# Second parts of the w_in weights from an adding transfer, in a hybrid delta-net and attention layer

## The chip, the cores and the metric

The kernel runs on one core of a Trainium2 chip. The metric is the device time of one execution in microseconds; lower is better. The core has a matrix engine (TensorE, PE in the profile; its weight loads are PEld), VectorE (DVE), ScalarE (ACT), GpSimd (POOL) and SyncE (SP), which issues most transfers. GpSimd and ScalarE can issue transfers too. Each engine works through its own queue in order.

## What is computed

One decoder layer for 1024 tokens of width 1024. A combined projection feeds two head groups, a gated delta rule and a differential attention; their outputs are projected back, and a gated feed-forward block follows.

```python
proj = rms_norm(h, norm1_w[l]) @ w_in[l]
dq, dk, dv, dz, da, db, fq, fk, fv = jnp.split(proj, IN_SPLITS, axis=-1)
qkv = jax.nn.silu(causal_dwconv(jnp.concatenate([dq, dk, dv], axis=-1), dn_conv_w[l]))
...
o_a = gated_delta_rule(q_a, k_a, v_a, g_a, beta_a).astype(h.dtype)
...
o_b = diff_attention(q_b, k_b, v_b, lam)
...
mix = jnp.concatenate([o_a.reshape(B_, S_, DN_V), o_b.reshape(B_, S_, DF_V)], axis=-1)
h = h + mix @ w_out[l]
u = causal_dwconv(rms_norm(h, norm2_w[l]) @ w_up[l], ffn_conv_w[l], ffn_conv_b[l])
gate, up = jnp.split(u, 2, axis=-1)
h = h + (jax.nn.silu(gate) * up) @ w_down[l]
```

## The kernel before, in words

Every large product is made of float32 operands split into two parts. The first part, `hi`, is a copy rounded to float32r (ScalarE, L202); the second part, `lo`, is what the rounding left, raw - hi. A product is then three matmuls: hi by hi, hi by lo, lo by hi. The normed input is split once into `xn`; the weights are split as they are loaded.

`split_w` makes the two parts of a loaded weight tile `raw` of 128 x 1024. With `lo_eng` G, GpSimd subtracts (L204); otherwise VectorE does (L206). `load_w128` loads one block of 128 columns of w_in (512 KB) and `gemm_T` uses it: two output halves of 512 tokens, eight k steps each, three matmuls per step (L422 and L423 read hi, L424 reads lo). `load_wn` loads 256 columns as two raw tiles of four k steps each, and `proj_nat` uses them: eight row blocks of 128 tokens, for each sixteen matmuls with hi (L403, L404) and then eight with lo (L406). Two row blocks share one PSUM tile, and there are two such tiles.

The order of use is this: the three blocks of head 0 of the delta group by `proj_T` (two of them loaded ahead into `pre`), then nine more by `delta_proj` for heads 1 to 3, then seven calls of `proj_nat` by 256 columns: one for dz ("dz1"), one for q and k of attention head 0, one for v, and four as `filler` within attention head 0. Between them, on the same engines, run the delta group's own chains: conv4 (L570 on ScalarE, three L573 on VectorE, L575 silu on ScalarE), the transposes L611, the scores L638 and L639, a triangular inverse by steps of VectorE (L684 to L687), and the scan over chunks (`delta_scan`, L754 to L776), in which TensorE, VectorE and ScalarE wait for each other in turn.

The weight parts `hi` and `lo` come from the pool wp with five buffers; a buffer comes free with TensorE's last matmul of the weight that it held. `raw` has three buffers; one comes free when both parts are made, and the next load on SP's queue waits for that.

The order of the instructions on each engine is written by a planner at build time: it goes by the priorities in `PRI` and by its own model of how long each instruction takes and when buffers come free. On the chip each engine keeps to that order.

The lines that the steps speak of, in `split_w`, are these (the functions around them follow):

```python
S.activation(hi, raw[:, 0:w], AF.Copy)
if lo_eng is G:
    G.tensor_tensor(lo, raw[:, 0:w], hi.bitcast(F32), op=ALU.subtract)
```

Of the kernel before, what the change touches and what calls it, by code (L numbers as in the profile page):

```python
# [10 lines left out]
F32 = mybir.dt.float32  # L11
# [3 lines left out]
AF = mybir.ActivationFunctionType  # L15
ALU = mybir.AluOpType
AX = mybir.AxisListType

P = 128
# [39 lines left out]
def hybrid_layer(ctx, tc, x, positions, norm1_w, w_in, dn_conv_w, dn_a_log, dn_dt_bias,  # L59
# [2 lines left out]
                 ffn_conv_b, w_down, cst, out, dbg=None, stop=None):  # L62
    nc = tc.nc
    V, S, G, PE = nc.vector, nc.scalar, nc.gpsimd, nc.tensor
    dbg = dbg or {}

    cp = ctx.enter_context(tc.tile_pool(name="cp", bufs=1))
# [14 lines left out]
    @contextmanager  # L82
    def part(name):
        p = tc.cur_priority
        q = max(0, p - PRI[name])
        tc.cur_priority = q
        yield
        tc.cur_priority = p + tc.cur_priority - q
# [3 lines left out]
    def nm(s):  # L92
        uid[0] += 1
        return f"{s}_{uid[0]}"
# [4 lines left out]
    def gtr(s):  # L99
        return gt(s, dt=F32R)  # L100

    def jt(s, dt=F32):
        return jp.tile([P, T], dt, tag="j", name=nm(s))

    def ct_(s, dt=F32):
        return cq.tile([P, T], dt, tag="c", name=nm(s))
# [13 lines left out]
    def psG(s="pG"):  # L120
        return pq.tile([P, 512], F32, tag="G", name=nm(s), bufs=2)
# [16 lines left out]
    win = w_in.rearrange("l d c -> (l d) c")  # L138
# [61 lines left out]
    def split_w(raw, lo_eng=None, w=T, alloc=None):  # L200
        hi, lo = ((alloc or wt)(s)[:, 0:w] for s in ("whi", "wlo"))
        S.activation(hi, raw[:, 0:w], AF.Copy)  # L202
        if lo_eng is G:
            G.tensor_tensor(lo, raw[:, 0:w], hi.bitcast(F32), op=ALU.subtract)  # L204
        else:
            V.tensor_tensor(lo, raw[:, 0:w], hi.bitcast(F32), op=ALU.subtract)  # L206
        return hi, lo

    def load_w128(w, c0, lo_eng=None, after=None):

        raw = rp.tile([P, T], F32, tag="raw", name=nm("raw"))
        if after is not None:
            G.tensor_copy(raw[:, 0:1], after)
        nc.sync.dma_start(raw.rearrange("p (k c) -> p k c", c=P),
                          w[:, c0:c0 + P].rearrange("(k p) c -> p k c", p=P))
        hi, lo = split_w(raw, lo_eng)
        return (hi.rearrange("p (k c) -> p k c", c=P), lo.rearrange("p (k c) -> p k c", c=P))

    def load_wn(srcs, lo_eng=None, kg=4, alloc=None, after=None):


        wd = sum(w for _, _, w in srcs)
        parts = []
        for k0 in range(0, NK, kg):
            n = min(kg, NK - k0)
            raw = rp.tile([P, T], F32, tag="raw", name=nm("raw"))
            if after is not None:
                V.tensor_copy(raw[:, 0:1], after)
            rv = raw[:, 0:n * wd].rearrange("p (k c) -> p k c", c=wd)
            o = 0  # L230
            for w, c0, w_ in srcs:
                nc.sync.dma_start(
                    rv[:, :, o:o + w_],
                    w[k0 * P:(k0 + n) * P, c0:c0 + w_].rearrange("(k p) c -> p k c", p=P))
                o += w_
            hi, lo = split_w(raw, lo_eng, n * wd, alloc)
            parts.append((hi.rearrange("p (k c) -> p k c", c=wd),
                          lo.rearrange("p (k c) -> p k c", c=wd)))
        return lambda kt: (parts[kt // kg][0][:, kt % kg, :], parts[kt // kg][1][:, kt % kg, :])
# [39 lines left out]
    def new_xn():  # L279

        return [tuple(xp.tile([P, 4 * T], F32R, tag="xn", name=nm("xn")) for _ in range(2))
                for _ in range(2)]

    def xs(xn, part, kt, a, b):
        q = a // 512
        return xn[q][part][:, kt * 512 + a - q * 512:kt * 512 + b - q * 512]
# [13 lines left out]
    xn = new_xn()  # L300
# [3 lines left out]
    with tc.manual_schedule(engines={mybir.EngineType.Activation}):  # L304
        for tt in range(NT + 1):
# [7 lines left out]
            if 0 < tt < 4:  # L313
                k = tt - 1
                n = min(3, NK - 3 * k)
                hi, lo = (gtr("w0")[:, 0:n * 264].rearrange("p (k c) -> p k c", c=264) for _ in range(2))
# [70 lines left out]
    def proj_nat(srcs, dst, lo_eng=None, extra=None):  # L387


        wf = load_wn(srcs, lo_eng, 4) if extra is None else lambda kt: tuple(t[:, kt % 3, :] for t in srcs[kt // 3])  # L390
        npt = 1 if extra is not None else 2
        for q in range(2):
            st = jt("pn")
            for t0 in range(0, 4, npt):
                ps = psG("pn")
                for i in range(npt):
                    tt = q * 4 + t0 + i
                    a, b = tt * P, tt * P + P
                    w = 264 if extra is not None else 256
                    o = ps[:, i * w:(i + 1) * w]  # L400
                    for kt in range(NK):
                        wh, wl = wf(kt)
                        PE.matmul(o, xs(xn, 0, kt, a, b), wh, start=kt == 0, stop=False)  # L403
                        PE.matmul(o, xs(xn, 1, kt, a, b), wh, start=False, stop=False)  # L404
                    for kt in range(NK):
                        PE.matmul(o, xs(xn, 0, kt, a, b), wf(kt)[1], start=False, stop=kt == NK - 1)  # L406
                if extra is not None:
                    V.tensor_copy(extra[:, tt, :], ps[:, 256:264])
                S.activation(st[:, t0 * 256:(t0 + npt) * 256], ps[:, 0:npt * 256], AF.Copy)
                yield  # L410
            nc.sync.dma_start(
                pn_dram[q * 512:(q + 1) * 512, dst:dst + 256].rearrange("(t p) c -> p t c", p=P),
                st.rearrange("p (t c) -> p t c", c=256))

    def gemm_T(w, c0, x_, ps, lo_eng, qq=(0, 1)):

        whi, wlo = pre.pop(c0 // P, None) or load_w128(w, c0, lo_eng)
        for q in qq:
            qs = (q * 512, q * 512 + 512)
            o = ps(q)  # L420
            for kt in range(NK):
                PE.matmul(o, whi[:, kt, :], xs(x_, 0, kt, *qs), start=kt == 0, stop=False)  # L422
                PE.matmul(o, whi[:, kt, :], xs(x_, 1, kt, *qs), start=False, stop=False)  # L423
                PE.matmul(o, wlo[:, kt, :], xs(x_, 0, kt, *qs), start=False, stop=kt == NK - 1)  # L424
            yield q, o
# [3 lines left out]
    def proj_T(h, kind):  # L429
        ct = kind * 4 + h  # L430
        st = praw[ct] = ct_("pT")
        for q, o in gemm_T(win, ct * P, xn, lambda q: psG("gT"), G):
            S.activation(st[:, q * 512:(q + 1) * 512], o, AF.Copy)
            yield

    def steps(gen, n=99):
        for _ in range(n):
            if next(gen, gen) is gen:
                break

    nat0 = proj_nat(wf0, 0, extra=dab)
    head0 = [proj_T(0, kind) for kind in (1, 0, 2)]
    steps(nat0, 4)
    steps(head0[0], 1)
# [18 lines left out]
    for bits in (8, 8, 8):  # L463
        e = math.floor(math.log2(abs(rest)))
        q = 2.0 ** (e - bits + 1)
# [115 lines left out]
    def load_rows(h):  # L581
        dec = gt("dec")
        nc.sync.dma_start(dec, G_dram[h:h + 1, :].broadcast_to([P, T]))
        return dec
# [379 lines left out]
                              og.rearrange("p (t c) -> p t c", c=P))  # L964

    def qk_proj(h):
        return proj_nat([(win, 2056 + h * P, P), (win, 2568 + h * P, P)], 512 + h * 256, G)

    def v_proj(pr):
        return proj_nat([(win, 3080 + pr * 256, 256)], 1536 + pr * 256, G)  # L970

    def delta_proj(h):
        for kind in (1, 0, 2):
            steps(proj_T(h, kind))

    def delta_end(d):
        with part("dscan"):
            delta_scan(d)
        with part("dout"):
            delta_out(d)  # L980

    ds_ = []
    for h in range(4):
        dec = load_rows(h)
        if h > 0:
            with part("dproj"):
                delta_proj(h)
            if h == 3:
                with part("dz1"):
                    steps(proj_nat([(win, 1792, 256)], 256, G))  # L990
        with part("dprep"):
            ds_.append(delta_prep(h, dec))
        if h > 0:
            delta_end(ds_[h - 1])
        with part("dinv"):
            delta_inverse(ds_[h])
# [8 lines left out]
    with part("qk0"):  # L1005
        steps(qk_proj(0))
# [5 lines left out]
    def load_wo(k0, c, eng, alloc=None):  # L1012

        parts = []
        for i in range(2):
            raw = rp.tile([P, T], F32, tag="raw", name=nm("raw"))
            r0 = (k0 + 2 * i) * P
            nc.sync.dma_start(raw.rearrange("p (k c) -> p k c", c=512),
                              wout[r0:r0 + 2 * P, c * 512:(c + 1) * 512].rearrange("(k p) c -> p k c", p=P))
            parts.append(split_w(raw, eng, T, alloc))  # L1020
        return lambda k: tuple(t[:, (k % 2) * 512:(k % 2) * 512 + 512] for t in parts[k // 2])
# [379 lines left out]
```

## Time and profile before

| | |
|---|---|
| median of 3 runs | 1429.08 us (1425.96 to 1431.47) |
| the profiled execution, its own time | 1430.1 us |
| its span, first to last instruction | 1428.4 us |
| mean granted TensorE clock | 0.975 |
| busy: PE, DVE, ACT, POOL | 1334.5, 878.3, 611.3, 377.0 us |
| wlo<-raw,whi on POOL (L204) | 34 instructions, 83.8 us |
| whi<-raw on ACT (L202) | 58 instructions, 61.0 us |

The span lies 1.7 us under the execution's own time. A busy time is the time in which an engine works on an instruction, whether or not anything waits for it; idle time of an engine that is not the bottleneck costs nothing. Times in the rows are counted from the start of the span.

### The profile page before, as it was taken

How to read it: one execution, taken by the hardware profiler on the slowest of the kernel's cores; microseconds unless marked ns; L12 is line 12 of the kernel's file. 1: busy time of each engine (PE TensorE's matmuls, PEld its weight loads, DVE VectorE, ACT ScalarE, POOL GpSimd, SP SyncE). 2: the span in 40 equal slices, each digit the busy share in tenths (PEclk: the TensorE clock that was granted, in tenths of full speed). 3: DMA queues.
4: the chain of work that ended last, by engine and by line, in shares of the span. 5: the costliest groups of instructions: out<-in, count | busy, mean ns of one | idle time of the engine just before them, and what ended most of it. 6: DMA issues, size and time to landing. Idle time of an engine off the chain costs nothing. (4 is left out here: it accounts for less than half of the span.)

```text
span 1428.4 us, 20608 instructions
## 1 busy us (share of the span) xinstructions
PE 1334.5 (93%) x7927; PEld 1126.6 (79%) x7927; DVE 878.3 (61%) x1745; ACT 611.3 (43%) x1086; POOL 377.0 (26%) x295
## 2 busy tenths in 40 slices
PE   7998898989989998999887999999999989999998
PEld 6876676888989986778665788888888868888887
DVE  5467978886342368867787666666666656334321
ACT  6445454533325365665554444444444435222220
POOL 3044313131242245240022434444333420000000
PEclk8999999999999999999998999999999999999999
DMA  7231112031543267455331222222222247547421
GB/s 225 83 80 35 34 39 75 17 113 66 162 109 116 88 169 192 105 134 162 123 121 29 89 74 89 85 78 89 89 74 82 82 137 243 195 149 229 139 88 59
DMA packets 143393, 155.14 MB, mean 109 GB/s; under 512 B 9279, under 2 KB 114367, under 8 KB 143295
## 3 DMA queue, kind: packets, MB, share of 16 engines
q1 hardware_dynamic: 130815, 144.14, 31.8%
q0 software_dynamic: 11008, 8.39, 3.1%
q8 instruction: 62, 1.02, 0.3%
q10 hardware_dynamic: 1472, 1.29, 0.3%
q14 instruction: 36, 0.29, 0.1%
HBM read 111.32 MB, written 38.29 MB: 105 GB/s over the span
## 5 line engine op out<-in xcount | busy, mean ns | idle before, releaser
L385 PE MATMUL pd<-whi,gl 128*128 128x512 f32 x352 | 137.0, 389 | 0.0
L383 PE MATMUL pd<-whi,gh 128*128 128x512 f32 x352 | 137.0, 389 | 0.0
L384 PE MATMUL pd<-wlo,gh 128*128 128x512 f32 x352 | 137.0, 389 | 0.0
L204 POOL TENSOR_TENSOR wlo<-raw,whi 128x1024 fp32r<-128x1024 f32 x34 | 83.8, 2471 | 194.1 <-PE gT L424 68.2
L1316 POOL TENSOR_TENSOR acc<-acc,acc 128x1024 f32<-128x1024 f32 x22 | 53.6, 2437 | 243.8 <-issue 215.5
L403 PE MATMUL pn<-whi,xn 128*128 128x256 f32 x448 | 116.3, 293 | 0.0
L404 PE MATMUL pn<-whi,xn 128*128 128x256 f32 x448 | 115.4, 291 | 0.0
L1339 ACT ACTIVATE gh<-act 128x1024 fp32r<-128x1024 f32 x42 | 44.6, 1061 | 123.9 <-PE pd L384 100.2
L1340 DVE TENSOR_TENSOR gl<-act,gh 128x1024 fp32r<-128x1024 f32 x42 | 52.0, 1241 | 68.9 <-ACT gh L1339 68.6
L403 PEld LDWEIGHTS pn<-whi,xn 128*128 128x128 f32 x448 | 87.3, 195 | 0.3
L404 PEld LDWEIGHTS pn<-whi,xn 128*128 128x128 f32 x448 | 87.0, 195 | 0.1
L202 ACT ACTIVATE whi<-raw 128x1024 fp32r<-128x1024 f32 x58 | 61.0, 1052 | 52.1 <-issue 18.3
L206 DVE TENSOR_TENSOR wlo<-rx,whi 128x1024 fp32r<-128x1024 f32 x22 | 28.9, 1315 | 82.6 <-ACT whi L202 82.3
L424 PE MATMUL gT<-xn,wlo 128*128 128x512 f32 x192 | 79.3, 413 | 0.0
L1230 PE MATMUL pa<-xT,whi 128*128 128x512 f32 x176 | 70.5, 400 | 9.3 <-ACT xT L1103 5.3
L422 PE MATMUL gT<-xn,whi 128*128 128x512 f32 x192 | 78.8, 410 | 0.0
L423 PE MATMUL gT<-xn,whi 128*128 128x512 f32 x192 | 78.6, 409 | 0.0
L202 ACT ACTIVATE whi<-rx 128x1024 fp32r<-128x1024 f32 x22 | 23.3, 1061 | 127.4 <-POOL rx L1271 127.4
L383 PEld LDWEIGHTS pd<-whi,gh 128*128 128x128 f32 x352 | 66.1, 188 | 13.8
L385 PEld LDWEIGHTS pd<-whi,gl 128*128 128x128 f32 x352 | 66.1, 188 | 13.7
L384 PEld LDWEIGHTS pd<-wlo,gh 128*128 128x128 f32 x352 | 66.1, 188 | 13.6
L206 DVE TENSOR_TENSOR wlo<-raw,whi 128x1024 fp32r<-128x1024 f32 x24 | 29.4, 1225 | 72.3 <-PE pd L384 53.1
(377 smaller groups left out, 3765.9 us busy)
## 6 DMA issues: line engine op xcount, KB each, us to landing
act<-act_dram SPq DMA_DIRECT2D x42, 512.0 KB, 4.5
rw<-in_w_up_dram SPq DMA_DIRECT2D x22, 512.0 KB, 3.8
act_dram<-acc SPq DMA_DIRECT2D x22, 512.0 KB, 2.6
raw<-in_w_down_dram SPq DMA_DIRECT2D x22, 512.0 KB, 4.4
raw<-in_w_in_dram SPq DMA_DIRECT2D x18, 512.0 KB, 4.0
pn_dram<-pn SPq DMA_DIRECT2D x16, 512.0 KB, 3.4
rx<-in_w_up_dram SPq DMA_DIRECT2D x22, 256.0 KB, 2.8
rz<-in_w_up_dram SPq DMA_DIRECT2D x22, 256.0 KB, 3.3
```

What stands on the lines that cost most here:

```text
L202: S.activation(hi, raw[:, 0:w], AF.Copy)
L204: G.tensor_tensor(lo, raw[:, 0:w], hi.bitcast(F32), op=ALU.subtract)
L206: V.tensor_tensor(lo, raw[:, 0:w], hi.bitcast(F32), op=ALU.subtract)
L383: PE.matmul(ps, lh, rh, start=first, stop=False)
L384: PE.matmul(ps, lh, rl, start=False, stop=False)
L385: PE.matmul(ps, ll, rh, start=False, stop=last)
L403: PE.matmul(o, xs(xn, 0, kt, a, b), wh, start=kt == 0, stop=False)
L404: PE.matmul(o, xs(xn, 1, kt, a, b), wh, start=False, stop=False)
L422: PE.matmul(o, whi[:, kt, :], xs(x_, 0, kt, *qs), start=kt == 0, stop=False)
L423: PE.matmul(o, whi[:, kt, :], xs(x_, 1, kt, *qs), start=False, stop=False)
L424: PE.matmul(o, wlo[:, kt, :], xs(x_, 0, kt, *qs), start=False, stop=kt == NK - 1)
L1230: PE.matmul(ps, wh[:, ks], xh[k], start=first, stop=False, skip_group_check=not start)
```

## The change

For 24 of the 34 weight tiles whose second part GpSimd made, ScalarE now writes the rounded copy a second time, with the sign turned, into `lo`; then GpSimd issues a transfer that adds `raw` into `lo` in place. The sum, raw - hi, is the same second part. The 24 are all the w_in blocks of `proj_T` that are loaded by it (10 tiles) and of the seven calls of `proj_nat` (14 tiles). The two tiles loaded ahead into `pre` and the eight tiles of w_out (`load_wo`) keep the subtraction.

```diff
+    DMA = nc.sync
...
     def split_w(raw, lo_eng=None, w=T, alloc=None):
         hi, lo = ((alloc or wt)(s)[:, 0:w] for s in ("whi", "wlo"))
         S.activation(hi, raw[:, 0:w], AF.Copy)
-        if lo_eng is G:
+        if lo_eng is DMA:
+
+            S.activation(lo, raw[:, 0:w], AF.Copy, scale=-1.0)
+            G.dma_start(lo.bitcast(F32), raw[:, 0:w], accum_op=ALU.add)
+        elif lo_eng is G:
             G.tensor_tensor(lo, raw[:, 0:w], hi.bitcast(F32), op=ALU.subtract)
...
-        for q, o in gemm_T(win, ct * P, xn, lambda q: psG("gT"), G):
+        for q, o in gemm_T(win, ct * P, xn, lambda q: psG("gT"), DMA):
...
-        return proj_nat([(win, 2056 + h * P, P), (win, 2568 + h * P, P)], 512 + h * 256, G)
+        return proj_nat([(win, 2056 + h * P, P), (win, 2568 + h * P, P)], 512 + h * 256, DMA)
...
-        return proj_nat([(win, 3080 + pr * 256, 256)], 1536 + pr * 256, G)
+        return proj_nat([(win, 3080 + pr * 256, 256)], 1536 + pr * 256, DMA)
...
-                    steps(proj_nat([(win, 1792, 256)], 256, G))
+                    steps(proj_nat([(win, 1792, 256)], 256, DMA))
```

`DMA` is only a mark that selects the branch; the adding transfer itself is issued by GpSimd.

## Rows read from the trace of the kernel before

**Rows 1.** The page, busy time of each engine: us, share of the span, instructions.

```profile
PE 1334.5 (93%) x7927; PEld 1126.6 (79%) x7927; DVE 878.3 (61%) x1745; ACT 611.3 (43%) x1086; POOL 377.0 (26%) x295
```

**Rows 2.** Stretches: start:end, length, busy by engine (PE, PEld, DVE, ACT, POOL), PE clock, DMA share, GB/s.

```profile
60.00:360.00 300.00, 269.47 (x2390) 227.71 (x2389) 229.47 (x627) 135.12 (x314) 82.96 (x62) 0.97 0.20 59
360.00:520.00 160.00, 153.13 (x1198) 148.00 (x1198) 64.33 (x155) 61.95 (x124) 50.24 (x39) 0.97 0.42 117
```

**Rows 3.** Who waited for GpSimd's wlo: TensorE's part, us and times.

```profile
  PE pn L406: 0.7, 1
```

**Rows 4.** TensorE timelines: start, us, instruction, count, [idle before <- what ended it].

```profile
109.90 1.33 PE L611 MATMUL pk<-k_sb,acc 128*128 128x128 f32 x5 [5.08 <-ACT acc L575]
...
122.10 1.16 PE L639 MATMUL pkq<-acc,acc 128*128 128x128 f32 x8 [1.54 <-DVE dec L645]
...
146.88 1.17 PE L611 MATMUL pk<-k_sb,acc 128*128 128x128 f32 x8 [3.21 <-ACT acc L575]
...
159.28 0.94 PE L639 MATMUL pkq<-acc,acc 128*128 128x128 f32 x6 [1.68 <-DVE dec L645]
...
246.11 0.49 PE L758 MATMUL pzz<-s,U 128*128 128x128 f32 x2 [2.15 <-DVE s L756]
...
267.58 0.49 PE L766 MATMUL pS<-s,kn 128*128 128x128 f32 x2 [1.74 <-DVE s L762]
...
309.31 0.49 PE L758 MATMUL pzz<-s,U 128*128 128x128 f32 x2 [1.89 <-DVE s L756]
...
315.93 0.49 PE L754 MATMUL pP<-s,acc 128*128 128x128 f32 x2 [1.56 <-DVE s L771]
...
430.76 1.50 PE L878 MATMUL pT<-k_sb,stk 128*128 128x128 f32 x7 [3.55 <-DVE stk L869]
```

**Rows 5.** VectorE and GpSimd timelines; the L573 line has min/median/max ns of all 36.

```profile
L573 DVE SCALAR_TENSOR_TENSOR acc<-pT,dcw,acc x36: 1268/1279/3433, 98.4 to 302.9; 128x1023 f32<-128x1023 f32 x12, 128x1022 f32<-128x1022 f32 x12, 128x1021 f32<-128x1021 f32 x12
...
135.37 10.23 DVE L573 SCALAR_TENSOR_TENSOR acc<-pT,dcw,acc 128x1023 f32<-128x1023 f32 x6
...
263.87 0.28 DVE L687 TENSOR_TENSOR inv<-inv 128x112 f32<-128x112 f32 x1
...
264.94 2.33 DVE L687 TENSOR_TENSOR inv<-inv 128x120 f32<-128x120 f32 x1
...
264.73 2.40 POOL L204 TENSOR_TENSOR wlo<-raw,whi 128x1024 fp32r<-128x1024 f32 x1 [9.01 <-PE gT L423]
```

**Rows 6.** The same two engines: L858 beside a subtraction, and beside two issued transfers.

```profile
424.26 2.52 DVE L858 TENSOR_TENSOR qk<-qk,cc 128x256 f32<-128x256 f32 x1
...
597.43 0.43 DVE L858 TENSOR_TENSOR qk<-qk,cc 128x256 f32<-128x256 f32 x1
...
596.81 1.59 POOL L1038 DMA_DIRECT2D mhl<-mT  x2
```

**Rows 7.** A stretch around the first gap; the clock is the third number from the end.

```profile
104.40:113.70 9.30, 4.22 (x15) 3.42 (x15) 5.35 (x6) 5.93 (x20) 0.00 (x0) 0.63 0.22 56
```

**Rows 8.** The DMA view, issues: queue, count, KB each, median us to landing.

```profile
raw<-in_w_in_dram SPq DMA_DIRECT2D x18, 512.0 KB, 4.0
...
mhl<-mT POOLq DMA_DIRECT2D x16, 256.0 KB, 5.3
K<-K POOLq DMA_DIRECT2D x32, 128.0 KB, 4.3
```

**Rows 9.** Timelines around the fourth call of proj_nat: SP, GpSimd, ScalarE, TensorE.

```profile
370.00 1.21 SPq L232 DMA_DIRECT2D raw<-in_w_in_dram  x2
...
391.12 4.77 POOL L204 TENSOR_TENSOR wlo<-raw,whi 128x1024 fp32r<-128x1024 f32 x2 [4.61 <-issue]
...
391.93 1.06 ACT L202 ACTIVATE whi<-raw 128x1024 fp32r<-128x1024 f32 x1 [4.20 <-PE pn L404]
...
392.64 0.28 PE L403 MATMUL pn<-whi,xn 128*128 128x256 f32 x1
...
395.94 0.74 PE L406 MATMUL pn<-wlo,xn 128*128 128x256 f32 x4 [0.73 <-POOL wlo L204]
```

## Prediction

> **What bounds the kernel now.** I read the page first. TensorE is busy for 93% of the span [rows 1], so a change pays only by removing TensorE idle time and costs only by making some. I then read the stretches in which the 24 changed subtractions run, about 69 to 490 us [rows 2]: from 60 to 360 us TensorE is idle for 300 - 269.5 = 30.5 us, VectorE is busy for 229.5 of 300; from 360 to 520 us it is idle for 6.9 us and the projections follow each other closely. GpSimd itself is at 83 of 300 us and is not the bound. For the result of a subtraction TensorE waits once, for 0.7 us [rows 3]. Judged by its own result alone, the subtraction is hidden.
>
> It is not hidden as a neighbour. I went through the idle times of TensorE before its instructions, and laid the timelines of VectorE and GpSimd beside each. Nine of them [rows 4] end with a VectorE chain in which one or two instructions are far longer than usual while a GpSimd subtraction runs. At 264.94 us a 120-column tensor_tensor of VectorE takes 2.33 us, the same line with 112 columns just before it 0.28; the subtraction beside it runs from 264.73 to 267.13, and the stretched instruction ends 0.14 us after it [rows 5]. TensorE needs what VectorE makes next (L762) and idles for 1.74 us. The conv chain is the same: six L573 take 10.23 us where six at their median of 1.28 would take 7.7 [rows 5]. So the subtraction holds up VectorE, VectorE holds up TensorE.
>
> **The change, part by part.** It removes 24 of the 34 GpSimd subtractions (10 in proj_T, 14 in proj_nat; the two loaded ahead in `pre` and the eight for w_out stay). It adds 24 ScalarE copies with scale -1, and 24 transfers of 512 KB issued by GpSimd that add raw into lo.
>
> Gain. Of each gap I take the smaller of the gap and the extension of the VectorE instruction that stands in its chain. For the two gaps behind L573 the extension is the smaller, 2.6 us each; for the other seven it is the gap: 1.54, 1.68, 2.15, 1.74, 1.89, 1.56 and 3.55 [rows 4] (the last has two instructions, L858 and L859, at about 2.5 us each where L858 otherwise takes 0.43 [rows 6]). The sum is 5.2 + 14.1 = 19.3 us. Next late after these are the same chains unstretched (ScalarE's silu, L575, behind the conv); I count them in by taking no more than the extension. Four of the gaps, the two of 5.08 and 3.21, that of 2.15 and that of 3.55, are followed by half clock: in the stretch around the first the granted clock is 0.63 [rows 7], which is 0.37 x 9.3 / 0.5 = 6.9 us at 1.2 GHz; the other three have about 3.4 us each, 17 in all. Work at half clock loses half its time, so 0 to 8.5 us come back; TensorE is idle or waits in much of it, so I take 3.
>
> Does the issue of the transfer hold up VectorE in turn? The rows say no: at 596.8 us GpSimd issues two transfers (1.59 us together), and L858 beside them takes 0.43 us, against 2.52 beside the subtraction [rows 6]. 24 issues at about 0.6 to 0.8 us replace 24 x 2.4 us of GpSimd [rows 5], which is idle then anyway.
>
> Cost: the second part comes later. Before, lo is ready 2.4 us after its buffer and hi are. After, it is 1.05 us of ScalarE (the duration of L202, same shape [rows 9]) and then the landing. No row shows an accumulating transfer, so the landing is unknown. From below, the plain SP load of the same 512 KB lands in 4.0 us; GpSimd's own transfers land in 4.3 us for 128 KB and 5.3 us for 256 KB (median) [rows 8]. An adding transfer must also read its destination, half as much movement again. From above I take 9 us, some 1.7 times the slowest of these medians. I choose 5.5, nearest to GpSimd's 256 KB. A landing gain over the subtraction is excluded by the 4.0.
>
> What this costs depends on how soon TensorE wants lo. Worked for the worst projection (the fourth): the two subtractions run from 391.12 to 395.89; TensorE begins with hi at 392.64 and wants lo's second half at 395.2, where it waits until 395.94 [rows 9]. After: hi is copied by 393.0 [rows 9], the negation by 394.05, issue 394.1, landing 399.6: 3.7 us later than 395.94. Without a stall the landing may be 1.8 us here. Read in the same way, the landing may be 4.6 us for the first changed weight (wanted at 75 us) and 6.6, 5.7, 2.5, 1.8, 7.0, 3.5 and 3.75 us for the seven calls of proj_nat from 265 us on; the other weights have 9 us or more. At 5.5 us the stalls are 0.9 + 0 + 0 + 3.0 + 3.7 + 0 + 2.0 + 1.75 = 11.4 us in the order of before; at 4.0 us 4.5, at 9 us 37. But the order is planned anew: with lo late, the hi matmuls of the next row blocks can go first, as two PSUM tiles of two row blocks each are there. I take half, 6 us.
>
> The Trainium skill has a price for this (DMA: Bandwidth & Descriptors, section "Anatomy of one DMA — SWDGE (gpsimd) path"): about 2.0 us and the bytes at 436 GB/s, an estimate of 3.2 us for 512 KB, for a plain transfer. By it the stalls would be 2 us in the order of before, about 1 after filling, and the total some 5 us lower than mine; the 4.3 us for 128 KB speak against it.
>
> Cost: ScalarE. 24 x 1.05 = 25 us on an engine that is busy for 135 + 62 of these 460 us [rows 2]. The negation waits on ScalarE for lo's buffer (five buffers in wp, freed by TensorE's last matmul of an earlier weight), where before GpSimd waited. Behind it in ScalarE's queue stand the copies out of PSUM (L409, L433), the silu of the conv and the scan's copies (L763, L776), for which TensorE and VectorE wait. If the planner places it well, it costs nothing; if every negation came in front of a needed copy, 25 us. I take 4, nearer to nothing, since ScalarE is idle for more than half of the stretch.
>
> Edits with one answer: raw is freed by the landing instead of by the subtraction, some 4 us later, so SP's next loads start later; the cover is that the first parts stand ready well before use (the weights wanted at 392.64 us are loaded from 370.00 on [rows 9]). If that cover is gone, the price is the same 4 us per weight. GpSimd's queue behind the transfer (L594, L673, the K copies L882) waits for ScalarE's negation as it waited for hi before: nothing.
>
> Sum: 1430.1 (the profiled run) - 19.3 - 3 + 6 + 4 = 1417.8. The median of the three runs, 1429.1, lies 1 us under the profiled one: 1417.
>
> **Rivals.** First, the idle time only moves. The planner writes a new order for all engines; the scan and conv chains run through ScalarE too, and ScalarE has more to do. Half the gain (11), full stalls (11.4) and 4 for ScalarE give +4: 1433. For it: VectorE remains busy for about 200 of 300 us. Against it: TensorE's gaps are tied one by one to stretched instructions.
>
> Second, slower: late landings. TensorE stalls at the start of each projection from 265 to 490 us, where wlo is wanted 1.8 to 7 us after the negation. With 9 us of landing and nothing to fill with: -22.3 + 37 + 4 = +19, 1448. It cancels the gain from a landing of 6.7 us, and costs 0.5% from 7.6 us. For it: transfers of GpSimd that meet other traffic already take over 5 us, and DMA share is 0.42 there [rows 2, 8]. Against it: the fill.
>
> Third, it doesn't do what it says: an adding transfer that holds up VectorE after all. Then no gain, +10: 1439. Against it: the two durations of L858 [rows 6].
>
> **How the numbers follow.** My forecast, 1417, has 0.55 with its own range of 1402 to 1421; the first rival 0.21; the second 0.16; the third 0.08. A measurement of this kernel can tell about 0.5%, 7 us, from no change: faster is under 1422, slower over 1436. So faster 0.55, same 0.21, slower 0.24. The low end: all 19.3, 8.5 for the clock and 1 for stalls, 1402, rounded to 1400. The high end takes in the first and third rival and the beginning of the second: 1441.
>
> **What would show it.** Right: no VectorE instruction of over 2 us in the conv and scan chains outside the remaining GpSimd work; TensorE idle from 60 to 360 us down from 30 to about 12 us; adding transfers landing in 5 to 6 us; few and short waits of L406 and L424 for DMA. Wrong: L406 waiting for DMA by several us at each projection (second rival); gaps of the old size behind L575, L762 or L756 with unstretched VectorE (first); stretched VectorE beside GpSimd's issue (third). An order far from that of before would make the term-by-term sum wrong even where each price holds.

## The result, and the profile after

The changed kernel takes 1439.24 us (median of 5 runs, 1436.36 to 1440.89) where the kernel before takes 1429.08: a ratio of 1.0068, 95% interval 1.0046 to 1.0089. It is slower by 10 us. That lies within the predicted range, 1400 to 1441, but the forecast was 1417 and faster. The profiled execution took 1439.78 us, its span is 1438.0.

Lines move by one in the changed kernel as far as the copy into hi, and by five behind the new branch of `split_w`: the copy into hi is L203, the negation L206 (ScalarE), the adding transfer L207 (GpSimd issues it), the remaining subtractions L209 (GpSimd) and L211 (VectorE). The conv's L573 is now L578, the first of its readers on TensorE L616 (before L611); the lo matmuls L406 and L424 are L411 and L429.

The page of after: busy time of each engine, one group of section 5 (operation, count, busy us, mean ns, idle time before and its releaser), and the queue through which GpSimd's transfers go (packets, MB, share of 16 engines). The last line is from the view of DMA issues.

```profile
PE 1339.8 (93%) x7927; PEld 1129.8 (79%) x7927; DVE 847.0 (59%) x1745; ACT 632.8 (44%) x1110; POOL 337.5 (23%) x295
...
q0 software_dynamic: 14464, 20.98, 7.9%
...
L411 PE MATMUL pn<-wlo,xn 128*128 128x256 f32 x448 | 73.8, 300 | 22.3 <-DMA wlo<-raw 22.2
...
wlo<-raw POOLq DMA_DIRECT2D x24, 512.0 KB, 4.6
```

Against [rows 1], VectorE lost 31 us of busy time and GpSimd 39.5, ScalarE gained 21.5: the work moved as meant. The third line is the answer to [rows 3]: where TensorE waited once, 0.7 us, for a subtraction, it now idles 22.2 us for the landing of adding transfers. A landing of 5 us means that the transfer has ended 5 us after its issue.

The answer to [rows 2], same stretches (start:end, length, busy of PE, PEld, DVE, ACT, POOL, PE clock, DMA share, GB/s):

```profile
60.00:360.00 300.00, 278.70 (x2475) 236.26 (x2474) 204.91 (x637) 153.13 (x339) 61.25 (x64) 0.98 0.34 85
360.00:520.00 160.00, 137.91 (x1035) 132.06 (x1034) 49.85 (x132) 61.13 (x113) 28.07 (x33) 0.94 0.58 145
```

TensorE's idle time from 60 to 360 us falls from 30.5 to 21.3 us, but from 360 to 520 us it rises from 6.9 to 22.1, and the clock there falls from 0.97 to 0.94 of full speed. Fixed times cut through different work, so the same view, cut where the work changes, says more: from TensorE's first matmul with a second part (L424, after: L429) to the last one of `proj_T`, and from there to the last one of `proj_nat` (L406, after: L411). Before, then after:

```profile
39.73:264.87 225.14, 204.59 (x1477) 166.64 (x1475) 163.09 (x465) 103.27 (x231) 62.58 (x46) 0.96 0.18 53
264.87:518.97 254.10, 237.35 (x2228) 225.94 (x2227) 138.70 (x361) 100.08 (x217) 69.59 (x55) 0.97 0.35 101
```

```profile
40.07:253.97 213.90, 202.03 (x1479) 164.06 (x1478) 141.11 (x466) 112.97 (x243) 43.40 (x45) 0.98 0.33 82
253.97:529.03 275.06, 243.53 (x2226) 230.62 (x2225) 128.52 (x360) 111.79 (x230) 49.72 (x55) 0.95 0.46 118
```

The matmul counts agree within two, so these are the same two pieces of work. The first became 11.2 us shorter, the second 21.0 us longer; what lies before and behind them is the same within 0.4 us. The change is two results in one: a gain and a larger loss. I call them the proj_T stretch and the proj_nat stretch. For each kernel their lengths, in us, with TensorE's idle time (length less busy) and the time at the lower of TensorE's two levels, 1.2 GHz (the other is 2.4), from the clock records. The lengths are those of the profiled execution alone; that of e1_T_only took 1423.0 us, 4 more than its median. Each ratio further down is to the kernel before as measured beside that variant, 1426.8 to 1430.2 us. e9_hold has 78 more of TensorE's matmuls in its first stretch than e1_T_only, e11_all_V and e12_act_dummy have 34 and 42 fewer than after (the others differ by ten at most), so for these three only the sum of both stretches compares.

| kernel | median us | proj_T stretch (idle, at 1.2 GHz) | proj_nat stretch (idle, at 1.2 GHz) |
|---|---|---|---|
| before | 1429.1 | 225.1 (20.5, 17.1) | 254.1 (16.8, 13.7) |
| after | 1439.2 | 213.9 (11.9, 6.8) | 275.1 (31.5, 27.3) |
| e1_T_only | 1418.7 | 217.3 (12.8, 13.7) | 254.1 (18.3, 13.7) |
| e2_nat_only | 1443.4 | 221.6 (19.4, 6.8) | 268.4 (27.0, 23.9) |
| e3_second_G | 1412.6 | 213.5 (10.2, 10.2) | 250.9 (14.6, 13.7) |
| e10_second_V | 1412.3 | 213.7 (10.3, 10.2) | 247.1 (11.9, 6.8) |
| e13_first_V | 1423.0 | 211.7 (11.6, 6.8) | 261.1 (22.8, 10.2) |
| e5_plain | 1406.4 | 211.6 (8.7, 10.2) | 244.3 (11.2, 3.4) |
| e9_hold | 1437.3 | 232.4 (21.9, 20.5) | 252.6 (15.3, 20.5) |
| e8_neg_gadd | 1439.3 | 230.7 (22.9, 20.5) | 255.8 (15.7, 23.9) |
| e7_T_dma_nat_dve | 1406.0 | 213.0 (11.3, 10.2) | 246.4 (11.0, 10.2) |
| e11_all_V | 1409.6 | 203.7 (8.6, 3.4) | 255.0 (14.3, 13.7) |
| e12_act_dummy | 1404.4 | 201.2 (8.1, 3.4) | 250.0 (10.2, 6.8) |

**The gain.** VectorE's conv in the proj_T stretch, GpSimd beside it, and TensorE's two waits behind the conv (timelines: start, us, instruction, count, idle before):

```profile
132.64 8.07 DVE L578 SCALAR_TENSOR_TENSOR acc<-pT,dcw,acc 128x1023 f32<-128x1023 f32 x6
```

```profile
137.69 0.91 POOL L207 DMA_DIRECT2D wlo<-raw  x1 [2.82 <-ACT wlo L206]
```

```profile
107.35 0.87 PE L616 MATMUL pk<-k_sb,acc 128*128 128x128 f32 x6 [2.62 <-ACT acc L580]
...
142.01 1.09 PE L616 MATMUL pk<-k_sb,acc 128*128 128x128 f32 x8 [1.43 <-ACT acc L580]
```

The six take 8.07 us, with the issue of an adding transfer at 137.69 beside them, where they took 10.23 [rows 5]; one of the six still takes 2.11, beside L599, GpSimd work that the change leaves. The two gaps behind the conv went from 5.08 and 3.21 us [rows 4] to 2.62 and 1.43. Over the whole trace, the VectorE instructions beside a subtraction of `split_w` took 38.8 us more before than if each had been as short as the shortest of its line and shape, and 7.8 us more after, beside the ten that remain; the 44 that run beside the issue of an adding transfer and no other GpSimd work took 0.2 us more. For the lines that hold the nine gaps of [rows 4], the waits of TensorE (line, releaser, us, times, longest), before and then after:

```profile
PE pk L611 <- ACT acc L575: 8.3, 2, 5.1
PE pT L878 <- DVE stk L869: 7.2, 4, 3.5
PE pzz L758 <- DVE s L756: 5.3, 3, 2.1
PE pS L766 <- DVE s L762: 4.0, 4, 1.7
PE pkq L639 <- DVE dec L645: 3.2, 2, 1.7
PE pP L754 <- DVE s L771: 3.1, 2, 1.6
...
PE pP L754 <- DVE s L769: 1.3, 1, 1.3
```

```profile
PE pT L883 <- DVE stk L874: 5.4, 4, 2.4
...
PE pk L616 <- ACT acc L580: 4.1, 2, 2.6
...
PE pP L759 <- DVE s L774: 2.9, 2, 1.6
...
PE pzz L763 <- DVE s L761: 1.9, 2, 1.3
...
PE pP L759 <- DVE s L776: 1.6, 1, 1.6
...
PE pS L771 <- DVE s L767: 0.6, 1, 0.6
```

32.4 us before, 16.5 after: pkq waits no more, pk, pzz and pS for half or less, pT for 1.8 us less, while pP waits as long as it did (4.4 and 4.5).

**The loss.** The second call of `proj_nat`: GpSimd issues the second tile's adding transfer, SP issues two transfers within 0.7 us of it, and TensorE waits:

```profile
298.88 0.85 POOL L207 DMA_DIRECT2D wlo<-raw  x1 [3.48 <-ACT s L768]
```

```profile
299.09 0.38 SPq L237 DMA_DIRECT2D raw<-in_w_in_dram  x1
299.57 0.46 SPq L416 DMA_DIRECT2D pn_dram<-pn  x1
```

```profile
307.20 1.22 PE L411 MATMUL pn<-wlo,xn 128*128 128x256 f32 x4 [4.51 <-DMA wlo<-raw]
```

The transfer was issued at 298.88 and TensorE could go on at 307.20, 8.3 us later. There are eight such waits, 22.2 us in all; six of them, 20.3 us, are for the second tile of a call. From 306.12 us, while TensorE still stands in this one, the granted clock is at 1.2 GHz, for 6.8 us:

```profile
306.12:312.95 6.83, 5.75 (x27) 5.75 (x28) 2.55 (x12) 0.73 (x2) 0.00 (x0) 0.50 0.86 239
```

Over the proj_nat stretch the time at 1.2 GHz grows from 13.7 to 27.3 us. Work in it takes twice as long, so up to half of the 13.6 us, 6.8, is lost. With the 14.7 us more of idle time that is 21.5, the 21.0 of the stretch.

### The profile page after: what moved, and what is told of

Same layout as the page of the kernel before. It is cut to its first block, busy times and chain, and to the rows that moved or that the text cites. A ratio compares the mean times of both kernels' runs of the same rounds, so it can differ in the third digit from the quotient of the medians.

```text
span 1438.0 us, 20654 instructions
## 1 busy us (share of the span) xinstructions
PE 1339.8 (93%) x7927; PEld 1129.8 (79%) x7927; DVE 847.0 (59%) x1745; ACT 632.8 (44%) x1110; POOL 337.5 (23%) x295
## 3 DMA queue, kind: packets, MB, share of 16 engines
q1 hardware_dynamic: 130815, 144.14, 31.5%
## 5 line engine op out<-in xcount | busy, mean ns | idle before, releaser
L408 PE MATMUL pn<-whi,xn 128*128 128x256 f32 x448 | 121.1, 301 | 1.3 <-ACT pn L414 1.3
L409 PE MATMUL pn<-whi,xn 128*128 128x256 f32 x448 | 120.0, 299 | 0.0
L411 PE MATMUL pn<-wlo,xn 128*128 128x256 f32 x448 | 73.8, 300 | 22.3 <-DMA wlo<-raw 22.2
L408 PEld LDWEIGHTS pn<-whi,xn 128*128 128x128 f32 x448 | 90.8, 203 | 1.8 <-ACT pn L414 1.5
L409 PEld LDWEIGHTS pn<-whi,xn 128*128 128x128 f32 x448 | 90.6, 203 | 0.2
L411 PEld LDWEIGHTS pn<-wlo,xn 128*128 128x128 f32 x448 | 62.8, 200 | 24.4 <-DMA wlo<-raw 24.1
L203 ACT ACTIVATE whi<-rx 128x1024 fp32r<-128x1024 f32 x22 | 23.4, 1061 | 127.2 <-POOL rx L1276 127.2
L429 PE MATMUL gT<-xn,wlo 128*128 128x512 f32 x192 | 78.3, 408 | 0.4 <-DMA wlo<-raw 0.4
L211 DVE TENSOR_TENSOR wlo<-rx,whi 128x1024 fp32r<-128x1024 f32 x22 | 29.0, 1317 | 82.8 <-ACT whi L203 82.2
L388 PEld LDWEIGHTS pd<-whi,gh 128*128 128x128 f32 x352 | 66.1, 188 | 13.6
L203 ACT ACTIVATE whi<-raw 128x1024 fp32r<-128x1024 f32 x58 | 60.9, 1050 | 33.1 <-issue 18.3
```

Source lines behind the costliest of these rows:

```text
L388: PE.matmul(ps, lh, rh, start=first, stop=False)
```

## The experiments

My theory after the result was: the gain is real and comes from GpSimd no longer holding up VectorE; the loss comes from landings that are later than TensorE wants them, above all of the second transfer of each proj_nat call. The rivals were ScalarE's added work, and a new order in which the idle time only moved.

**One part alone.** e1_T_only uses the adding transfer for the ten proj_T tiles, e2_nat_only for the fourteen proj_nat tiles; the rest goes back to GpSimd's subtraction (in e1_T_only the calls for v and dz1 too, which the cut leaves out).

```diff
 e1_T_only:
-        return proj_nat([(win, 2056 + h * P, P), (win, 2568 + h * P, P)], 512 + h * 256, DMA)
+        return proj_nat([(win, 2056 + h * P, P), (win, 2568 + h * P, P)], 512 + h * 256, G)
...
 e2_nat_only:
-        for q, o in gemm_T(win, ct * P, xn, lambda q: psG("gT"), DMA):
+        for q, o in gemm_T(win, ct * P, xn, lambda q: psG("gT"), G):
```

> The adding transfer for the ten proj_T tiles alone; the fourteen proj_nat tiles go back to GpSimd's subtraction. Theory A (the two halves of the change are independent: in the proj_T stretch VectorE is freed, which gains 10.9 us up to the last L424 matmul, 264.9 to 254.0 us; in the proj_nat stretch the second transfer of each pair lands too late, which costs 21 us): 1418 us, +-4, with the last proj_T matmul at about 254 us and the stretch from there to the last proj_nat matmul back at about 254 us. Rival B (the time came from the new order of all engines and from ScalarE's negations, wherever they are): between 1426 and 1440, and the two stretches don't separate.

> The adding transfer for the fourteen proj_nat tiles alone; the ten proj_T tiles go back to GpSimd's subtraction. Theory A: no gain in the first stretch (last proj_T matmul at about 265 us) and the whole loss in the second (about 275 us long, TensorE waiting 20 us or more for wlo's transfers): 1450 us, +-4. Rival B: between 1429 and 1442.

e1_T_only: 1418.69 us, ratio 0.9939 (0.9922 to 0.9955), TensorE waits 0.3 us for a landing. Faster, as the theory had it: 7.8 us in the proj_T stretch and 0 in the other, in the profiled execution. e2_nat_only: 1443.43 us, ratio 1.0113 (1.0097 to 1.0129). Its direction fits; the size falls between the two theories, since its proj_nat stretch grew by 14.3 us and not by 21. The wait is this one (line, releaser, us, times, longest):

```profile
PE pn L411 <- DMA wlo<-raw: 17.9, 9, 4.6
```

**Only the second tile taken back.** e3_second_G gives the second tile of each proj_nat call to GpSimd's subtraction, e10_second_V to VectorE's.

```diff
 e3_second_G:
-            hi, lo = split_w(raw, lo_eng, n * wd, alloc)
+            hi, lo = split_w(raw, G if lo_eng is DMA and k0 else lo_eng, n * wd, alloc)
...
 e10_second_V:
-            hi, lo = split_w(raw, lo_eng, n * wd, alloc)
+            hi, lo = split_w(raw, None if lo_eng is DMA and k0 else lo_eng, n * wd, alloc)
```

> As the change, but the second tile of each proj_nat pair keeps GpSimd's subtraction, so no adding transfer follows another closely. Theory A (the loss is the second transfer's landing of 7 to 8.5 us, behind the first one's): the first transfers land in about 4.6 us as before, TensorE's waits for wlo fall from 22 us to under 7, and the time is 1418 to 1425. Rival B (the negation on ScalarE or the new order costs it): waits of another kind take their place and the time stays above 1433.

> As the change, but the second tile of each proj_nat pair is subtracted by VectorE (1.23 us) instead of by a second adding transfer. Theory A: first transfers of 4.6 us alone, few waits for wlo, seven holds fewer than with GpSimd: 1407 to 1414, below the 1412.6 of the version with GpSimd's second part. Rival B (VectorE's own 8.6 us of work falls on the scan's chain): 1414 to 1420.

e3_second_G: 1412.6 us, ratio 0.9901 (0.9876 to 0.9926), faster than the theory's 1418 to 1425; e10_second_V: 1412.3, ratio 0.9877 (0.9853 to 0.99). Seven transfers of 24 taken back turn a loss of 10 us into a gain of 14 to 18. In e3_second_G all seventeen landings lie between 4.5 and 5.2 us and TensorE waits 1.8 us for them; in e10_second_V it waits 4.3. So the seven second transfers are the loss.

**The addition itself.** e5_plain issues the same 24 transfers without adding: `lo` then holds raw and not the second part, so this kernel doesn't compute the layer, but its transfers move the same bytes.

```diff
-            G.dma_start(lo.bitcast(F32), raw[:, 0:w], accum_op=ALU.add)
+            G.dma_start(lo.bitcast(F32), raw[:, 0:w])
```

> As the change, but the transfer copies raw over lo and doesn't add, so lo holds the wrong part; all instructions and sizes are otherwise the same. Theory C (the addition makes the transfer slow, as it must also read its destination): landings fall from 4.6 us alone and 7 to 8.5 us for the second of a pair to about 4 and 6, and the time falls by 8 us or more, to 1431 or less. Theory A (the pair's two transfers share the same DMA engines, whatever they do): landings within 0.5 us of these, and 1439 +-4.

It takes 1406.37 us (one execution, no interval). Its view of tile wlo (min, median, max), its wait of TensorE and its queue, and as a third the queue of e11_all_V, which issues none of the 24:

```profile
DMA to landing us min/median/max: 2.8/2.9/5.5
...
PE pn L411 <- DMA wlo<-raw: 2.9, 2, 1.7
...
q0 software_dynamic: 14464, 20.98, 5.4%
```

```profile
q0 software_dynamic: 11008, 8.39, 3.1%
```

The same view of after has 4.5/4.6/8.5. The addition makes a transfer of the same bytes 1.7 us later at the median, and it holds the DMA engines about twice as long: (7.9% - 3.1%) x 1438 / 24 = 2.9 us of all 16 engines for each adding transfer, (5.4% - 3.1%) x 1405 / 24 = 1.35 us for each plain one. That the landings would stay within 0.5 us without the addition fell; they came down further than to the other theory's 4 and 6 us. The prediction's "half as much movement again" was short as well: the engines are held about twice as long. By the Trainium skill (DMA: Bandwidth & Descriptors, section "Anatomy of one DMA — SWDGE (gpsimd) path") a transfer takes about 2.0 us and its bytes at 436 GB/s, an estimate of 3.2 us for 512 KB. The plain transfer's median of 2.9 us agrees with it, the adding one's 4.6 does not. The prediction set the 3.2 us aside because of the 4.3 us for 128 KB; the plain transfer's 2.9 shows that this reason didn't carry over, and that what the estimate lacks is the addition.

**Why the second one.** In e13_first_V VectorE subtracts the first tile of each call, and only the second is made by the transfer, so no two adding transfers are open together.

```diff
-            hi, lo = split_w(raw, lo_eng, n * wd, alloc)
+            hi, lo = split_w(raw, None if lo_eng is DMA and not k0 else lo_eng, n * wd, alloc)
```

> In the changed kernel the second adding transfer of each proj_nat call lands in 6.8 to 8.5 us, all others in 4.5 to 5.2. Two theories of why. Pair: it shares the engines with the first one. Loads: it shares them with the load of the next raw tile, which the landing of the first one (that frees a raw buffer) lets SP issue, and with the store of a finished row half. Here the first tile of each call is subtracted by VectorE and only the second is made by the adding transfer, so no two adding transfers are open together, while loads and stores stay. Pair: the seconds land in 4.5 to 5.2 us, TensorE waits for them for under 4 us in all, 1408 to 1416 us. Loads: the seconds still take 6 us and more where a load or store is issued meanwhile, TensorE waits for 8 us or more, 1416 to 1432 us.

1423.04 us, ratio 0.9973 (0.9953 to 0.9993), TensorE waiting 12.9 us in six waits: the time and the waits that the loads theory expected. Its landings came only in part: without a partner the seconds land in 4.9 to 7.2 us, two of the seven in 6 or more. The longest, with a load of a raw tile still open for 3.5 us and a store of a finished row half issued 0.2 us after it, and the wait at its end:

```profile
380.00 0.91 POOL L207 DMA_DIRECT2D wlo<-raw  x1 [4.67 <-ACT wlo L206]
```

```profile
380.21 0.37 SPq L416 DMA_DIRECT2D pn_dram<-pn  x1
```

```profile
387.21 1.07 PE L411 MATMUL pn<-wlo,xn 128*128 128x256 f32 x4 [3.92 <-DMA wlo<-raw]
```

Neither theory holds alone. In after, the seconds of calls 2 and 3 were issued over 4 us behind the firsts, as these landed, and still took 8.3 and 7.1 us: they share their start with a load of the next raw tile, which SP issues 0.05 us after the first one's landing has freed a buffer, and with a store or another load. Those of calls 4 to 7, 0.7 to 1.9 us behind the firsts, took 6.8 to 8.5; that of call 5 has no other company than its first within 4 us, and took 6.8. The firsts, behind which the second comes 0.7 us later or more, took 4.5 to 5.2. So in this kernel all six late ones have company at their start: an adding transfer still open on GpSimd's queue, or a load or a store within 0.7 us. Without the pair 12.9 of the 22.2 us of waiting remain. Company alone doesn't decide it: in e2_nat_only the seconds of calls 2 and 3, with a store or a load issued 0.5 and 0.7 us after them, landed in 5.5 and 5.6 us, and in e13_first_V one with a load issued 0.7 us before it in 5.0. Which company counts, and how much, isn't settled. e14_rb4, the changed kernel with four raw buffers, was to show whether earlier loads help; it has no result, since its buffers don't fit into SBUF (a pool needs 8.6 KB per partition where 4.7 are left).

**Is it the hold on VectorE?** e9_hold is e1_T_only with the subtraction put back as idle work: GpSimd first subtracts into lo, then the negation overwrites it and the transfer adds.

```diff
+            G.tensor_tensor(lo, raw[:, 0:w], hi.bitcast(F32), op=ALU.subtract)
             S.activation(lo, raw[:, 0:w], AF.Copy, scale=-1.0)
             G.dma_start(lo.bitcast(F32), raw[:, 0:w], accum_op=ALU.add)
```

> The adding transfer for the ten proj_T tiles alone, as in the run of that name, but GpSimd also does its old subtraction first, into the same lo, which the negation then overwrites: its result is not used. Theory A (the gain comes from VectorE no longer being held up while GpSimd reads SBUF): the long VectorE instructions come back beside the ten subtractions, and the time goes back by about what the proj_T half gained, from 1418.7 to 1426 or more. Rival B (the gain came from the new order of the engines or from GpSimd's shorter queue behind the weights): 1417 to 1422, with the gaps of TensorE still gone.

1437.3 us, ratio 1.0059 (1.0038 to 1.008), against 1418.7 of e1_T_only. Both stretches together, e9_hold and then e1_T_only:

```profile
39.04:524.08 485.04, 447.77 (x3702) 396.47 (x3701) 295.95 (x825) 212.33 (x457) 141.40 (x110) 0.96 0.33 88
39.29:510.74 471.45, 440.37 (x3702) 391.19 (x3701) 281.02 (x825) 211.14 (x457) 114.27 (x100) 0.97 0.33 91
```

The same matmuls take 13.6 us longer, while TensorE waits 2.2 us for landings. Its idle time is 37.3 us against 31.1 in e1_T_only, and 37.3 is also what the kernel before has: the subtractions bring back all the idle time that their absence had saved. VectorE and GpSimd side by side:

```profile
97.90 10.24 DVE L579 SCALAR_TENSOR_TENSOR acc<-pT,dcw,acc 128x1023 f32<-128x1023 f32 x6
```

```profile
100.50 2.98 POOL L206 TENSOR_TENSOR wlo<-raw,whi 128x1024 fp32r<-128x1024 f32 x1 [0.36 <-POOL dec L600]
```

The conv is back at 10.24 us. The subtraction's result is thrown away, so what it costs is what it does to its neighbours, and a little through the later start of the negation and the transfer. The rest of the 13.6 us goes with the clock: 41.0 us at 1.2 GHz against 27.3, and half of the 13.7 us more is lost. The kernel before has 30.7 us at 1.2 GHz; so e9_hold is slower than that one with the same idle time, and why it is longer at the lower clock isn't shown. The Trainium skill (SBUF — State Buffer, section "Who interferes with whom") says that a VectorE instruction with two inputs in SBUF contends with a GpSimd instruction that reads SBUF. The trace agrees: 2.33 us against 0.28 for L687 [rows 5].

**Is it ScalarE?** e8_neg_gadd keeps the negation and lets GpSimd add raw in place of the transfer; e12_act_dummy lets VectorE add; e11_all_V lets VectorE subtract with no negation (`None` selects that branch).

```diff
 e8_neg_gadd:
-            G.dma_start(lo.bitcast(F32), raw[:, 0:w], accum_op=ALU.add)
+            G.tensor_tensor(lo, raw[:, 0:w], lo.bitcast(F32), op=ALU.add)
...
 e12_act_dummy:
-            G.dma_start(lo.bitcast(F32), raw[:, 0:w], accum_op=ALU.add)
+            V.tensor_tensor(lo, raw[:, 0:w], lo.bitcast(F32), op=ALU.add)
...
 e11_all_V: DMA becomes None in proj_T and in the calls of proj_nat
```

> ScalarE's negation as in the change, for all 24 tiles, but GpSimd adds raw to it with an instruction instead of a transfer. This leaves the added ScalarE work and its waits for buffers as the only difference to the kernel before. Theory A (ScalarE's part costs next to nothing): 1428 to 1433, with TensorE's waits for wlo under 5 us. Rival B (the negations on ScalarE, 25 us of work, and their waits for buffers hold up the copies out of PSUM): 1436 or more.

> All 24 tiles by VectorE's subtraction (1.23 us each), no adding transfer, no negation, no GpSimd. Theory A (GpSimd's reading holds VectorE for 2.4 us a tile, so VectorE doing it itself is held for half as long; and ScalarE's negation costs 6 us in the proj_T stretch, which falls away): 1404 to 1418, the proj_T stretch, from its first to its last lo matmul, between 210 and 222 us against 225 before. Rival B (29 us of own work on VectorE is as bad as being held): 1424 or more.

> As the run with all 24 tiles by VectorE, with ScalarE's negation kept: VectorE adds raw to it. The difference to that run is ScalarE's part alone (24 copies of 1.05 us and their waits for buffers) without GpSimd and without transfers. Theory A (ScalarE's part costs some 6 to 9 us, as the version with GpSimd's addition showed): 6 to 10 us above that run. Rival B (those 9 us were an effect of GpSimd's later start): within 3 us of that run.

e8_neg_gadd: 1439.32 us, ratio 1.0057 (1.0036 to 1.0078), so the same GpSimd time with ScalarE's 24 negations is slower than before, which looked like a price of ScalarE. The pair e11_all_V (1409.61, ratio 0.9864, 0.9846 to 0.9883) and e12_act_dummy (1404.36, ratio 0.982, 0.9802 to 0.9837) says otherwise: there the same 24 negations come on top and the time is 5 us shorter. That ScalarE's part costs 6 to 10 us fell, though the rival's "within 3 us" wasn't met either. The busy time in the profiled execution of e8_neg_gadd, whose span is 1440.3 us:

```profile
PE 1345.7 (93%) x7927; PEld 1136.2 (79%) x7927; DVE 872.5 (61%) x1745; ACT 633.3 (44%) x1110; POOL 376.4 (26%) x295
```

TensorE is idle for 1440.3 - 1345.7 = 94.6 us, and for 93.9 in the kernel before: it doesn't wait longer. But it is at 1.2 GHz for 96.3 us against 72.3; half of the 24 us, 12, is the 11.9 by which the span is longer. Why this order leaves it so much longer at the lower clock stays open. Of the 11.9, 5 us lie behind the last changed weight, where the work is the same as before. That last stretch is between 905.7 and 914.6 us long in these kernels, so a new order from the planner alone moves it by some 5 us, and smaller differences between kernels here aren't explained.

**The transfer in proj_T alone, VectorE elsewhere.** e7_T_dma_nat_dve keeps the transfer in proj_T, where landings have slack, and lets VectorE subtract in proj_nat.

```diff
-        return proj_nat([(win, 2056 + h * P, P), (win, 2568 + h * P, P)], 512 + h * 256, DMA)
+        return proj_nat([(win, 2056 + h * P, P), (win, 2568 + h * P, P)], 512 + h * 256, None)
```

> The adding transfer for the ten proj_T tiles; the fourteen proj_nat tiles by VectorE's subtraction (1.23 us each in the traces) instead of GpSimd's 2.4. Theory A (VectorE held up by GpSimd's reading costs time, and proj_nat needs lo early): no DMA waits, no holding, lo ready 1.2 us after hi: 1408 to 1416. Rival B (17 us more of work on VectorE in the scan's stretch costs as much as the holding did): 1418 or more.

1406.0 us, ratio 0.983 (0.9802 to 0.9858), a little below the 1408 to 1416 of the theory. It and e12_act_dummy beat both kernels by over 20 us and can't be told apart by these intervals; nor can it be from e11_all_V. That the transfer is better in proj_T than VectorE's subtraction isn't shown.

## Why the prediction was wrong, step by step

**GpSimd's subtraction holds up VectorE, and VectorE holds up TensorE: right, and about the size.** The forecast took back 19.3 us of gaps; the waits of these lines fell by 32.4 - 16.5 = 15.9. The gap before L754 (1.56) is the plain miss among them: its line waits as long as before. The one of 3.55 before L878 is still 1.75 at 426.17 us, with VectorE's L863 and L864 (before L858 and L859) back at 0.43 and 0.42. In the proj_T stretch five of the nine stood, 10.6 us, and idle time there fell by 8.6. e9_hold puts the subtractions back and brings idle time back to what it was before.

**The issue of a transfer doesn't hold up VectorE: right.** The third rival, 1439 us, gave the number that came, by a mechanism that didn't. The issues take 0.87 us each, and VectorE beside them was 0.2 us longer in 44 instructions.

**The landing: the step that failed.** The term "the second part comes later" stood at 6 us in the sum; the waits are 22.2 + 0.4 = 22.6 us. Of the 16.6 us between them, 11.1 come from the landings and the rest from the halving below. The forecast gave all 24 transfers one landing, 5.5 us, taken from GpSimd's 256 KB transfers. The typical adding transfer is faster than that, 4.6, and those are not the ones that matter. The seven second tiles took 4.7, 8.3, 7.1, 7.6, 6.8, 7.8 and 8.5 us, where the working itself allowed 6.6, 5.7, 2.5, 1.8, 7.0, 3.5 and 3.75; the first changed weight took 5.0, allowed 4.6. The working's own list with these landings is 0.4 + 0 + 2.6 + 4.6 + 5.8 + 0 + 4.3 + 4.8 = 22.5 us, against 11.4 with 5.5 us for all. TensorE's waits in the same order are 0.4, 0, 4.5, 2.8, 4.1, 2.3, 4.1 and 4.5: the two sums agree, but calls miss by up to 2.3 us, so the agreement is in part luck. The way of working it out holds; the one landing for all did not. [rows 2] showed a DMA share twice as high from 360 us on as before, and the second rival said so, but its price of 9 us was for a transfer that is slow in general; that the late ones would be those that are wanted first stood nowhere.

**The halving for other matmuls that fill: wrong, 5.5 us of the miss.** The planner hardly did it. In calls 2, 5, 6 and 7 TensorE does the sixteen hi matmuls of the first row block, and then waits without doing any of the next one. Only in calls 3 and 4 does it take hi matmuls of the next row block first, four and sixteen of them, and it still waits 2.8 and 4.1 us there, where the list has 4.6 and 5.8.

**Half clock: the sign was turned.** The forecast got 3 us back. The proj_T stretch did give back (17.1 to 6.8 us at 1.2 GHz), but beside each of the five waits of over 2.6 us in the proj_nat stretch stands a time at 1.2 GHz, 3.4 or 6.8 us long, 27.3 us in all where it was 13.7.

**ScalarE, 4 us: no such cost was seen.** e12_act_dummy is faster than e11_all_V with the negations on top. A new order alone moves some 5 us, so a smaller cost can't be excluded.

The sum again: 1430.1 - 19.3 - 3 + 22.5 + 0 = 1430.3, and the half clock behind the new waits adds at most 6.8: 1437. That is 3 us short of the profiled 1439.8, within what a new order moves. With the measured 15.9 in place of 19.3, and the clock of the proj_T stretch (10.3 us less at 1.2 GHz, at most 5.1 back) in place of 3, it is 1438.4.

**The rivals.** The second, late landings, is what happened: a loss at the start of each projection, wanted 1.8 to 7 us after the negation, with nothing to fill. The forecast gave it 0.16 and 1448 us; it came out cheaper because the transfers that TensorE waits for landed in 4.6 to 8.5 us and not in 9, for 22.6 us of waiting and not 37. That the time lies within the stated range is luck: its upper end, 1441, took in the first and the third rival, which didn't happen, and of the second only the beginning. The first rival, that the idle time only moves, would have kept gaps of the old size behind unstretched VectorE work; of these only the 1.56 before L754 and half of that before L878 are seen.

## What to carry to other kernels

Price an elementwise instruction of GpSimd by what it does to VectorE beside it: 24 subtractions on an engine that was idle anyway cost this kernel more than VectorE's doing them itself, at 1.2 us each (1429.1 us against 1409.6). Price a transfer that replaces it one by one, not by a median: in this kernel the late ones were those with company, and where TensorE wants the data first there is company, since the same moment frees buffers and lets loads start (calls 2 and 3). Where the second part had 5 us or more to spare the adding transfer did no harm (e1_T_only, e7_T_dma_nat_dve); where it is wanted at once, VectorE was better (e10_second_V, e7_T_dma_nat_dve). And look at the clock beside the idle time: two kernels with the same idle time were 12 us apart (e8_neg_gadd and the kernel before).

## What the runs showed of the hardware

An adding transfer of 512 KB within SBUF lands 4.5 us after its issue at best, a plain one 2.8 (after, e5_plain). By the queue's share it holds the 16 DMA engines for 2.9 us against 1.35. With other transfers open at its start, or issued within 0.7 us, it lands in up to 8.5 us, a plain one in up to 5.5. Its issue takes GpSimd 0.87 us against 0.55 for the plain one, and 44 VectorE instructions beside such issues were 0.2 us longer in all, where those beside 34 subtractions of GpSimd were 38.8 us longer.
